# Engine order planned by free SBUF places and new DMA landing times, and the transposed input of the second block fetched from the SP queue

## The chip, the cores and the metric

The kernel runs on one core of a Trainium2 chip. The metric is device time in microseconds (us) of one execution. Three runs of the kernel before gave a median of 1719.25 us (1719.18 to 1719.7).

## What is computed

Two transformer blocks run one after the other on 512 tokens of width 2048, all in float32. The first block puts 16 meta tokens in front (528 rows), takes an RMS norm, multiplies by a 2048-row input weight, runs eight heads of grouped attention with rotary angles and eight heads of differential attention, gates both, multiplies by an output weight, norms and adds the residual. The second block norms that sum and multiplies by its own input weight; its columns feed eight heads of stick-breaking attention and a linear recurrence (convolution, two gates, a scan), and an output weight and a residual follow:

```
x = first_block(x, meta_tokens, ...)       # h + rmsnorm(y @ w_out)
return second_block(x, ...)                # proj = rmsnorm(x) @ w_in_2 ; ... ; h + y @ w_out_2
```

## The kernel before, in words

**Matmuls.** A float32 operand is split into two float32r parts, high and low, and a product is three passes over them (`PASSES`, L667). `split` (L417 to L419) makes the parts: ACT casts the high part (L418), DVE subtracts for the low one (L419). All matmuls are recorded on one line, L451.

**Weights.** Weights of the plain products (`in_wp`) come in units of two halves, 512 KB a half, through three raw places (`wraw`) and three split places (`wsp`). `load_next` (L570) issues the load of a half from the SP queue (L580) and splits it. Most other projections use a seven-product scheme over a pair of column blocks (`seven`, `produce`, `sum_up`), whose weights are loaded by SP (L616) and partly summed by a DMA that POOL issues (L625).

**Between the blocks.** `side_pair` (L1291) norms two token tiles, transposes them on TensorE, scales them into `xg` (L1316), stores `xg` to the DRAM tensor `x2d` with a DMA of POOL (L1319) and splits it into `big`. Then `v_half` (L1696) multiplies two token tiles at a time by the value weights of the second block, plain units; its result goes through ACT (L1703) to the DRAM tensor `vd` by a DMA of POOL (L1704). Meanwhile `side_x2` (L938) prepares the operands of the seven-product scheme: for each of six pairs (j, 6 + j) it fetches two transposed 128 x 512 blocks of `x2d` into tiles of the tag `e` (L945), 256 KB each in pieces of 512 B, subtracts quarters on DVE (L951 to L954) and splits the results with ACT and DVE into `x23b` and `x1sb`. The fetch of pair j + 1 is written ahead of the work on pair j. The tag `e` has six places, which many other steps use too. Later, L1782 fetches blocks of `x2d` of half that size from the SP queue.

**The order of the work.** TensorE's order comes from generators that `run` interleaves by a clock of their own. For the other engines (ACT, DVE, POOL and the SP queue) the class `Plan` records every instruction with its cost and its predecessors, gives each a due time counted back from the TensorE instruction that needs it (`order`, L253), runs a list scheduler over all engines and lays the result down as a fixed order on each engine. An engine works strictly in that order: an instruction that waits holds up all that stand behind it. `own` (L128) ties a tile to the tag whose places it uses; in the kernel before, the first use of a tile has all users of the tile `bufs` places back in its tag as hard predecessors:

```
if len(h) > bufs:
    before.append(h[-1 - bufs])
...
cost, busy = (1300.0 + nb / 260.0, 60.0) if e == "SP" else (3300.0 + nb / 220.0, 870.0)
```

The tile allocator itself gives a tile any place of its tag that is free.

Of the kernel before, what the change touches and what calls it, by code (L numbers as in the profile page):

```python
# [16 lines left out]
P = 128  # L17
# [93 lines left out]
class Plan:  # L111
# [2 lines left out]


    HOP = 40.0
    LEAD, SETTLED = 8000.0, 60000.0
    TABLES = ({"Tanh", "Exp", "Square", "Identity", "Copy"}, {"Exp", "Ln", "Abs", "Square", "Identity", "Copy"},
              {"Sqrt", "Square", "Identity", "Copy"})

    def __init__(self):
        self.ins, self.engine, self.cost, self.busy, self.func, self.preds = [], [], [], [], [], []
        self.nbytes, self.adds = [], []
        self.parts, self.users, self.after_of, self.history = {}, {}, {}, {}
        self.turn_of, self.opened, self.newest, self.begun = {}, {}, {}, []
        self.behind, self.names = None, {}

    def own(self, ap, tag, bufs, following=()):  # L128

        h = self.history.setdefault(tag, [])  # L130
        self.turn_of[ap.name] = tag
        h.append(ap.name)
        before = list(following)
        if len(h) > bufs:
            before.append(h[-1 - bufs])
        self.after_of[ap.name] = before
        self.users[ap.name] = []
        return ap

# [38 lines left out]
    def __call__(self, ins):  # L178
        op, e = type(ins).__name__[4:], str(ins.engine).split(".")[-1]
        aps = [[o.bass_ap for o in group if hasattr(o, "bass_ap")] for group in (ins.outs, ins.ins)]  # L180
        if not type(ins).__name__.startswith("Inst") or (not aps[0] and op != "LoadActFuncSet"):
            return
        i = len(self.ins)
        preds, begun = set(), set()
        if self.behind is not None and str(self.behind.engine) == str(ins.engine):
            preds.add(self.behind.name)
        preds = {self.names[p] for p in preds} if preds else set()
        pe = e == "PE"
        for writes, group in ((False, aps[1]), (True, aps[0])):
            for ap in group:  # L190
                name = ap.name
                if name.startswith("in_") or name.startswith("out_"):
                    continue
                for t in self.after_of.pop(name, ()):
                    preds.update(self.users.get(t, ()))
                if name in self.turn_of:
                    tag = self.turn_of.pop(name)
                    if tag in self.newest:
                        begun.add(self.newest[tag])
                    self.newest[tag] = self.opened[name] = i  # L200
                elif name in self.opened:
                    begun.add(self.opened[name])
                if name in self.users:
                    self.users[name].append(i)
                span = self._span(ap)
                w = writes or str(ap.space) == "PSUM"
                parts = self.parts.setdefault(name, {})
                lo, hi = span[0][0], span[-1][1]
                for key in [k for k in parts if k[0][0] < hi and lo < k[-1][1]]:
                    if not any(a < d and c < b for a, b in key for c, d in span):  # L210
                        continue
                    writer, readers = parts[key]
                    if writer is not None:
                        preds.add(writer)
                    if w:
                        preds.update(readers.values())
                        if key == span or (len(span) == 1 and lo <= key[0][0] and key[-1][1] <= hi):
                            del parts[key]
                if w:
                    parts[span] = [i, {}]  # L220
                else:
                    parts.setdefault(span, [None, {}])[1]["PE" if pe else i] = i
        preds.discard(i)
        if pe:
            preds = {j for j in preds if self.engine[j] != "PE"}
            begun = {j for j in begun if self.engine[j] != "PE"}
        self.begun.append(begun - preds - {i})
        n = max([ap.free_size() for g in aps for ap in g] or [1])
        self.nbytes.append(0)
        self.adds.append(str(getattr(ins, "cce_op", "")).endswith("add"))  # L230
        if op == "DMACopy":
            nb = 4
            for _, k in aps[0][0].ap:
                nb *= k
            self.nbytes[-1] = nb
            cost, busy = (1300.0 + nb / 260.0, 60.0) if e == "SP" else (3300.0 + nb / 220.0, 870.0)
        elif op == "LoadActFuncSet":
            cost = busy = 1283.0
        else:
            if op == "TensorScalarPtr" and getattr(ins, "is_tensor_tensor_scan", False):  # L240
                op = "TensorTensorScan"
            if pe:
                n = aps[0][0].free_size()
            cost, busy = self._costs(ins, e, op, n, str(aps[1][0].dtype) if aps[1] else "")
        self.ins.append(ins)
        self.names[ins.name] = i
        self.engine.append(e)
        self.cost.append(cost)
        self.busy.append(busy)
        self.func.append(str(getattr(ins, "func", "")).split(".")[-1] if op == "Activation" else op)  # L250
        self.preds.append(preds)

    def order(self):  # L253

        N = len(self.ins)
        succs = [[] for _ in range(N)]
# [7 lines left out]
        t, due = 0.0, [math.inf] * N  # L264
# [3 lines left out]
                t += self.busy[i]  # L268
        for i in range(N - 1, -1, -1):
            if self.engine[i] != "PE":  # L270
                due[i] = min([due[j] for j in succs[i]] + [t]) - self.cost[i] - self.HOP
                due[i] = min([due[i]] + [due[j] for j in heirs[i]])
        left = [len(p) + len(b) for p, b in zip(self.preds, self.begun)]
        at = [0.0] * N
        clock = {e: 0.0 for e in self.engine}
        ready = {e: [] for e in clock}
# [8 lines left out]
        def wanted(i):  # L285
            now = due[pe[min(pe_next, len(pe) - 1)]]
            return not self.nbytes[i] or now > self.SETTLED or due[i] - self.LEAD <= now

        eager = False
        while count < N:  # L290
            best = None
            for e, r in ready.items():
                if e == "PE":
                    if pe_next == len(pe) or left[pe[pe_next]]:
                        continue
                    i = pe[pe_next]
                    s = max(clock[e], at[i])
                else:
                    r = [i for i in r if eager or wanted(i)]
                    if not r:  # L300
                        continue
                    s = max(clock[e], min(at[i] for i in r))
                if best is None or s < best[0]:
                    best = (s, e)
            if best is None:
# [3 lines left out]
            if e == "PE":  # L309
                i = pe[pe_next]  # L310
                pe_next += 1
            else:
                def rank(i):
                    other = e == "Activation" and self.ins[i] and self.switch(i, table[0])
                    return due[i] + (4000.0 if other else 0.0)

                i = min((i for i in ready[e] if at[i] <= s and (eager or wanted(i))), key=rank)
                eager = False
                ready[e].remove(i)
            if e == "Activation":  # L320
# [6 lines left out]
            clock[e] = s + self.busy[i]  # L327
            end = s + self.cost[i]
            if self.nbytes[i]:
                lat = 1300.0 if e == "SP" else 2400.0  # L330
                pipe = max(clock[e] + lat / 2, pipe) + self.nbytes[i] * (1.9 if self.adds[i] else 1.0) / 300.0
                end = pipe + lat / 2
            self.fin[i] = end
            done[e].append(i)
            count += 1
            for j, when in [(j, end + self.HOP) for j in succs[i]] + [(j, s) for j in heirs[i]]:
                left[j] -= 1
                at[j] = max(at[j], when)
                if not left[j] and self.engine[j] != "PE":
                    ready[self.engine[j]].append(j)  # L340
# [10 lines left out]
def hybrid_two_block_kernel(ctx: ExitStack, tc: tile.TileContext, wp, wq, wc, xT, xtok, par, lvec, cst, rg, pg, lruw, out):  # L351
    nc = tc.nc
# [61 lines left out]
    def blocks(ap, n=P):  # L414
        return ap.rearrange("p (a b) -> p a b", b=n)
# [522 lines left out]
    def side_x2():  # L938
# [3 lines left out]
        def fetch(j):  # L942
            x = et(NTOK), et(NTOK)
            for t, kt in zip(x, (j, KS + j)):
                pool.dma_start(blocks(t), x2d[kt // 8].rearrange("t p c -> p t c")[:, :, kt % 8 * P : (kt % 8 + 1) * P])  # L945
            return x

        a, b = fetch(0)
# [1035 lines left out]
```

## Time and profile before

| | us |
|---|---|
| median of three runs | 1719.25 |
| the profiled execution | 1719.21 |
| span of its trace, first to last instruction | 1717.4 |
| TensorE (PE) busy | 1668.4 |
| DVE busy | 1207.1 |
| ACT busy | 945.4 |
| POOL busy | 188.2 |

The mean granted clock of TensorE is 0.992 of full speed. An engine's time in the span is busy time plus idle time; in the rows a figure in square brackets is the idle time just before an instruction and what ended it. "issue" stands for time in which the engine waited for nothing that the profile shows. A DMA's instruction on its queue is short; "to landing" runs from the issue to the last byte's semaphore.

### The profile page before, as it was taken

The page shows a single profiled execution, that of the slowest core. Times are in us where ns is not written, and L with a number is a line of the kernel's source. Part 1 is how long each engine was busy: PE and PEld are TensorE (multiplying, and loading weights), DVE is VectorE, ACT ScalarE, POOL GpSimd, SP SyncE. Part 2 cuts the span into 40 slices and gives each one's busy share as a digit, 9 for nine tenths or more (in the row PEclk, how much of TensorE's full clock was granted, in tenths as well). Part 3 has the DMA queues.
Part 4 walks back from the last instruction along what each step waited for, and adds up shares of the span by engine and source line. Part 5 has one row for each costly group of instructions (what it writes and reads, how often), then busy time and mean ns, then how long its engine had stood idle before and what let it go on. Part 6 is the DMA issues. An engine that isn't in the chain of part 4 may idle for free.

```text
span 1717.4 us, 28307 instructions
## 1 busy us (share of the span) xinstructions
PE 1668.4 (97%) x10840; PEld 1512.0 (88%) x10840; DVE 1207.1 (70%) x2073; ACT 945.4 (55%) x1581; POOL 188.2 (11%) x217
## 2 busy tenths in 40 slices
PE   8999999999999999999999879999999999999999
PEld 8789999999999999888887659999998888888887
DVE  4874787776889888873577647898875466886433
ACT  6554566664767766673455434666643366775311
POOL 0111121111122222100000111111100000000000
PEclk9999999999999999999999989999999999999999
DMA  8535856767665656544577666666667322434233
GB/s 301 174 124 141 209 136 165 175 158 168 145 145 140 153 129 144 149 132 134 200 249 257 233 188 163 154 188 151 190 173 239 114 85 86 141 93 126 83 92 129
DMA packets 104552, 273.01 MB, mean 159 GB/s; under 512 B 11728, under 2 KB 19024, under 8 KB 102736
## 3 DMA queue, kind: packets, MB, share of 16 engines
q1 hardware_dynamic: 86944, 221.90, 39.7%
q0 software_dynamic: 17472, 49.29, 16.2%
q8 instruction: 85, 1.39, 0.3%
q14 instruction: 51, 0.42, 0.1%
HBM read 241.79 MB, written 29.36 MB: 158 GB/s over the span
## 4 chain that ended last, share of the span: by engine, by line
PE 63%; DVE 5%; DMA 3%; issue 3%; ACT 2%; POOL 0%; SPq 0%; DVEq 0%; ACTq 0%; POOLq 0%
PE pj L451 56%; PE pmt L451 2%; PE pss L451 2%; DVE wsp L419 2%; DMA wraw<-in_wp 1%; PE ptt L454 1%; DMA wraw<-in_wq 1%; PE bank L451 1%; ACT wsp L418 1%; PE pmt L454 1%; DMA e<-x2d 0%; DMA vd<-e 0%; PE pss L454 0%; DVE ar L1276 0%; POOL e L945 0%
## 5 line engine op out<-in xcount | busy, mean ns | idle before, releaser
L451 PE MATMUL pj<-wsp,big 128*128 128x512 f32 x3072 | 745.6, 400 | 23.9 <-ACT wsp L418 18.3
L451 PEld LDWEIGHTS pj<-wsp,big 128*128 128x128 f32 x3072 | 575.7, 190 | 159.1 <-ACT wsp L418 20.6
L419 DVE TENSOR_TENSOR wsp<-wraw,wsp 128x768 fp32r<-128x768 f32 (+3 forms) x459 | 464.1, 1016 | 231.7 <-ACT wsp L418 224.5
L418 ACT CAST wsp<-wraw 128x768 fp32r<-128x768 f32 (+3 forms) x459 | 401.6, 878 | 385.8 <-PE pj L451 291.3
L451 PE MATMUL pj<-big,wsp 128*128 128x264 f32 (+2 forms) x4224 | 539.2, 283 | 10.6 <-ACT wsp L418 7.2
L451 PEld LDWEIGHTS pj<-big,wsp 128*128 128x128 f32 x4224 | 518.6, 189 | 13.6 <-ACT wsp L418 7.5
L625 POOL DMA_DIRECT2D wraw<-in_wq x104 | 90.8, 883 | 631.1 <-DVE wsp L419 496.4
L451 PE MATMUL pj<-x,wsp 128*128 128x264 f32 x720 | 100.8, 287 | 3.2 <-DVE wsp L419 1.9
L451 PEld LDWEIGHTS pj<-x,wsp 128*128 128x128 f32 x720 | 92.4, 188 | 4.8 <-DVE wsp L419 2.5
L451 PE MATMUL pj<-x1s,wsp 128*128 128x264 f32 (+1 forms) x576 | 78.0, 285 | 1.9 <-DVE e L1760 1.9
L418 ACT CAST pt<-ptt 128x512 fp32r<-128x512 f32 (+2 forms) x96 | 50.7, 528 | 51.5 <-PE ptt L454 51.2
L419 DVE TENSOR_TENSOR pt<-ptt,pt 128x512 fp32r<-128x512 f32 (+2 forms) x96 | 59.6, 621 | 25.9 <-ACT pt L418 25.1
L451 PE MATMUL pss<-kk,qq 128*128 128x264 f32 x448 | 72.1, 289 | 3.6 <-DVE vtail L999 1.9
L451 PEld LDWEIGHTS pj<-x1s,wsp 128*128 128x128 f32 x576 | 72.9, 188 | 2.2 <-DVE e L1760 2.1
L451 PE MATMUL pmt<-pt,vv 128*128 128x256 f32 (+1 forms) x528 | 69.3, 279 | 0.0
L451 PEld LDWEIGHTS pmt<-pt,vv 128*128 128x128 f32 x528 | 67.2, 188 | 1.5
L1231 ACT ACTIVATE e<-e,sm 128x528 f32<-128x528 f32 x64 | 47.2, 737 | 38.2 <-DVE sm L1228 37.9
L451 PEld LDWEIGHTS pss<-kk,qq 128*128 128x128 f32 x448 | 61.4, 188 | 6.1 <-PE ptt L454 2.3
L451 PE MATMUL pj<-y,wsp 128*128 128x256 f32 x432 | 55.6, 282 | 0.0
L451 PEld LDWEIGHTS pj<-y,wsp 128*128 128x128 f32 x432 | 53.4, 189 | 0.0
L454 PE MATMUL ptt<-ident,e 128*128 128x128 f32 x336 | 52.5, 273 | 0.0
L1228 DVE CUSTOM_DVE_ANT_0 e<-pss,ar 128x528 f32<-128x528 f32 x64 | 44.9, 702 | 6.0 <-PE pss L451 5.8
(285 smaller groups left out, 1549.8 us busy)
## 6 DMA issues: line engine op xcount, KB each, us to landing
wraw<-in_wp SPq DMA_DIRECT2D x167, 512.0 KB, 4.1
wraw<-in_wq SPq DMA_DIRECT2D x128, 384.0 KB, 3.9
wraw<-in_wq POOLq DMA_DIRECT2D x104, 384.0 KB, 5.2
wraw<-in_wc SPq DMA_DIRECT2D x64, 256.0 KB, 2.8
gated<-e SPq DMA_DIRECT2D x40, 256.0 KB, 3.2
e<-in_xT SPq DMA_DIRECT2D x28, 264.0 KB, 4.2
early<-in_xtok SPq DMA_DIRECT2D x4, 1024.0 KB, 8.1
e<-yd SPq DMA_DIRECT2D x16, 256.0 KB, 4.0
```

The costliest lines, as they stand in the source:

```text
L418: act.copy(hi, src)
L419: dve.tensor_tensor(lo, src, f(hi), ALU.subtract)
L451: _queue(nc.tensor.matmul(out, lhsT, rhs, start=start, stop=stop).ins, cost)
L454: _queue(nc.tensor.transpose(out, in_, identity).ins, 110.0)
L625: pool.dma_start(pair_raw[(p, r)], wq[p, q], accum_op=ALU.add)
L1228: dve.tensor_tensor_reduce(out=halves(x), in0=s[:, :, :HL], in1=halves(bias[:, b0 : b0 + L]), scale=1.0, scalar=3e38, op0=ALU.add, op1=ALU ...
L1231: act.activation(x, x, AF.Exp, scale=-1.0, bias=nm, accum_out=l[:, m : m + 1])
```

## The change

Four things are edited.

- Places: the first use of a tile no longer has the users of the tile `bufs` back as predecessors. The scheduler keeps, for each tag, the times at which its places come free (a place is taken at a tile's first use and freed 40 ns after its last user ends); an instruction that opens a tile starts no earlier than the first free place, and not at all while none is free. The due times still look at the tile `bufs` back (`soft`).
- DMA model: a DMA of SP lands after 1900 ns of latency (1300 before), one of POOL after 2000 ns (2400 before), 700 ns more where the target is DRAM, plus the bytes over a shared pipe at 300 bytes per ns as before.
- Margin: whoever needs a DMA's data is planned up to 700 ns after its modelled landing, where its due time leaves room (half of the slack).
- `side_x2` issues its twelve fetches (L945) from SP instead of POOL.

```diff
@@ class Plan
-    LEAD, SETTLED = 8000.0, 60000.0
+    LEAD, SETTLED, MARGIN = 8000.0, 60000.0, 700.0
...
@@ own
-        before = list(following)
+        self.after_of[ap.name] = list(following)
+        self.room[tag], self.tag_of[ap.name] = bufs, tag
         if len(h) > bufs:
-            before.append(h[-1 - bufs])
-        self.after_of[ap.name] = before
+            self.heir_of[ap.name] = h[-1 - bufs]
...
@@ __call__
+                    self.opens.setdefault(i, []).append(name)
+                    if name in self.heir_of:
+                        self.soft.setdefault(i, []).extend(self.users[self.heir_of[name]])
...
-            cost, busy = (1300.0 + nb / 260.0, 60.0) if e == "SP" else (3300.0 + nb / 220.0, 870.0)
+            lat = (1900.0 if e == "SP" else 2000.0) + (700.0 if str(aps[0][0].space) == "DRAM" else 0.0)
+            self.lat[i] = lat
+            cost, busy = (lat + nb / 260.0, 60.0) if e == "SP" else (lat + 870.0 + nb / 150.0, 870.0)
...
@@ order
-                due[i] = min([due[j] for j in succs[i]] + [t]) - self.cost[i] - self.HOP
+                due[i] = min([due[i], min([due[j] for j in succs[i]] + [t]) - self.cost[i] - self.HOP])
                 due[i] = min([due[i]] + [due[j] for j in heirs[i]])
+            for j in self.soft.get(i, ()):
+                if self.engine[j] != "PE":
+                    due[j] = min(due[j], due[i] - self.cost[j] - self.HOP)
+        free = {tag: [0.0] * n for tag, n in self.room.items()}
...
+        def slot(i):
+            t = 0.0
+            for name in self.opens.get(i, ()):
+                f = free[self.tag_of[name]]
+                t = max(t, min(f) if f else math.inf)
+            return t
...
-                    s = max(clock[e], min(at[i] for i in r))
+                    s = max(clock[e], min(max(at[i], slot(i)) for i in r))
+                    if s == math.inf:
+                        continue
...
-                i = min((i for i in ready[e] if at[i] <= s and (eager or wanted(i))), key=rank)
+                i = min((i for i in ready[e] if max(at[i], slot(i)) <= s and (eager or wanted(i))), key=rank)
...
-                lat = 1300.0 if e == "SP" else 2400.0
+                lat = self.lat[i]
...
+            for name in self.opens.get(i, ()):
+                f = free[self.tag_of[name]]
+                f.remove(min(f))
+            for name in tiles[i]:
+                live[name] -= 1
+                last[name] = max(last.get(name, 0.0), end + self.HOP)
+                if not live[name]:
+                    free[self.tag_of[name]].append(last[name])
...
+                if self.nbytes[i] and when > s:
+                    late = clock["PE"] - due[pe[min(pe_next, len(pe) - 1)]]
+                    when += min(max((due[j] + late - when) / 2, 0.0), self.MARGIN)
...
@@ side_x2, fetch
-                pool.dma_start(blocks(t), x2d[kt // 8].rearrange("t p c -> p t c")[:, :, kt % 8 * P : (kt % 8 + 1) * P])
+                nc.sync.dma_start(blocks(t), x2d[kt // 8].rearrange("t p c -> p t c")[:, :, kt % 8 * P : (kt % 8 + 1) * P])
```

## Rows read from the trace of the kernel before

**Rows 1.** The page, busy time, its share of the span and instructions.
```profile
span 1717.4 us, 28307 instructions
PE 1668.4 (97%) x10840; PEld 1512.0 (88%) x10840; DVE 1207.1 (70%) x2073; ACT 945.4 (55%) x1581; POOL 188.2 (11%) x217
```

**Rows 2.** Waits of PE, whole span: waiter, awaited: us in total, times, longest us.
```profile
PE pj L451 <- ACT wsp L418: 26.7, 9, 6.8
PE pj L451 <- DVE wsp L419: 7.0, 11, 1.6
```

**Rows 3.** Busy time by stretch: PE, PEld, DVE, ACT, POOL, PEclk, DMA share, GB/s.
```profile
0.00:50.00 50.00, 42.81 (x313) 41.18 (x314) 22.60 (x39) 32.47 (x47) 0.83 (x7) 1.00 0.83 307
...
1700.00:1717.00 17.00, 13.20 (x57) 10.35 (x56) 4.62 (x7) 1.05 (x1) 0.00 (x0) 0.97 0.24 93
```

**Rows 4.** The same view, stretches cut to the stages.
```profile
970.00:1020.00 50.00, 31.94 (x102) 22.60 (x101) 24.89 (x44) 16.10 (x24) 8.31 (x12) 0.80 0.48 147
1020.00:1044.00 24.00, 24.00 (x105) 19.42 (x105) 12.17 (x10) 11.02 (x13) 2.02 (x3) 1.00 0.70 208
...
720.00:730.00 10.00, 7.09 (x21) 5.09 (x20) 7.89 (x13) 7.75 (x13) 0.00 (x0) 0.66 0.58 190
895.00:915.00 20.00, 18.10 (x85) 14.27 (x84) 15.41 (x27) 9.38 (x13) 1.22 (x3) 1.00 0.90 353
```

**Rows 5.** Timeline of PE from 970 to 1020: start, us, instruction, idle before.
```profile
980.11 1.22 PE L451 MATMUL pj<-wsp,big 128*128 128x512 f32 x2 [6.78 <-ACT wsp L418]
...
996.23 1.22 PE L451 MATMUL pj<-wsp,big 128*128 128x512 f32 x2 [4.67 <-ACT wsp L418]
...
1015.82 1.22 PE L451 MATMUL pj<-wsp,big 128*128 128x512 f32 x2 [5.27 <-ACT wsp L418]
```

**Rows 6.** Waits of all engines from 955 to 1020.
```profile
ACT x1s L418 <- DVE e L951: 32.0, 6, 7.9
POOL e L945 <- issue: 29.2, 8, 5.9
DVE e L951 <- DMA e<-x2d: 26.5, 6, 6.4
...
POOL e L945 <- DMA vd<-e: 6.1, 1, 6.1
```

**Rows 7.** Timeline of POOL from 940 to 1050: first, one in the middle and last fetch.
```profile
959.25 0.78 POOL L945 DMA_DIRECT2D e<-x2d  x1 [0.37 <-PE pj L451]
...
976.92 0.76 POOL L945 DMA_DIRECT2D e<-x2d  x1 [2.96 <-issue]
...
1009.88 0.76 POOL L945 DMA_DIRECT2D e<-x2d  x1 [2.90 <-issue]
```

**Rows 8.** Line L945, its twelve fetches on POOL.
```profile
DMA to landing us min/median/max: 3.3/3.4/6.4
```

**Rows 9.** Fetches of half the size on SP: timeline at 1293 to 1300, line L1782.
```profile
1294.79 4.03 SPq L1782 DMA_DIRECT2D e<-x2d  x6
...
DMA to landing us min/median/max: 4.8/5.5/6.2
```

**Rows 10.** Tile wraw from 955 to 1020: durations in ns, min/median/max.
```profile
L419 DVE TENSOR_TENSOR wsp<-wraw,wsp x14: 1215/1218/1227, 954.7 to 1017.7; 128x1024 fp32r<-128x1024 f32 x14
...
L418 ACT CAST wsp<-wraw x13: 1037/1043/1053, 955.2 to 1016.2; 128x1024 fp32r<-128x1024 f32 x13
...
DMA to landing us min/median/max: 3.5/4.4/7.0
```

**Rows 11.** The page, DMA issues: count, KB each, median us to landing.
```profile
wraw<-in_wp SPq DMA_DIRECT2D x167, 512.0 KB, 4.1
...
wraw<-in_wq POOLq DMA_DIRECT2D x104, 384.0 KB, 5.2
```

**Rows 12.** Timeline of PE, the two longest gaps outside 970 to 1020 and the start.
```profile
722.54 0.73 PE L451 MATMUL pj<-wsp,big 128*128 128x512 f32 x1 [2.30 <-ACT big L418]
...
1234.81 2.42 PE L451 MATMUL pj<-x1s,wsp 128*128 128x256 f32 x18 [1.85 <-DVE e L1760]
```

More of the change, by code (lines that the diff above doesn't have):

```diff
@@ L122, in __init__ @@
         self.ins, self.engine, self.cost, self.busy, self.func, self.preds = [], [], [], [], [], []
-        self.nbytes, self.adds = [], []
+        self.nbytes, self.adds, self.lat = [], [], {}
         self.parts, self.users, self.after_of, self.history = {}, {}, {}, {}
@@ L126, in __init__ @@
         self.behind, self.names = None, {}
+        self.room, self.tag_of, self.heir_of, self.opens, self.soft = {}, {}, {}, {}, {}
     def own(self, ap, tag, bufs, following=()):
@@ L270, in order @@
             if self.engine[i] != "PE":
-                due[i] = min([due[j] for j in succs[i]] + [t]) - self.cost[i] - self.HOP
+                due[i] = min([due[i], min([due[j] for j in succs[i]] + [t]) - self.cost[i] - self.HOP])
                 due[i] = min([due[i]] + [due[j] for j in heirs[i]])
+            for j in self.soft.get(i, ()):
+                if self.engine[j] != "PE":
+                    due[j] = min(due[j], due[i] - self.cost[j] - self.HOP)
+        free = {tag: [0.0] * n for tag, n in self.room.items()}
+        live, last, tiles = {}, {}, [[] for _ in range(N)]
+        for name, us in self.users.items():
+            live[name] = len(set(us))
+            for i in set(us):
+                tiles[i].append(name)
+        def slot(i):
[4 more added lines that the diff above has]
+            return t
         left = [len(p) + len(b) for p, b in zip(self.preds, self.begun)]
@@ L296, in order @@
                     i = pe[pe_next]
-                    s = max(clock[e], at[i])
+                    s = max(clock[e], at[i], slot(i))
+                    if s == math.inf:
+                        continue
                 else:
@@ L301, in order @@
                         continue
-                    s = max(clock[e], min(at[i] for i in r))
+                    s = max(clock[e], min(max(at[i], slot(i)) for i in r))
+                    if s == math.inf:
+                        continue
                 if best is None or s < best[0]:
```

## The prediction

> **What bounds the kernel now.** I began with the page's busy times: TensorE works 1668.4 of 1717.4 us [rows 1], so the kernel is bound by TensorE and only the 49.0 us of its gaps, and what a lowered clock costs after them, can be won. The waits of PE come next: 26.7 us in nine gaps end with an ACT cast of a weight, 7.0 us in eleven with the DVE subtract behind it [rows 2]. So it is late weights, not late results, that stop TensorE.
>
> Busy time by stretch says where. The start holds 50 - 42.81 = 7.19 us of gaps and the tail 17 - 13.20 = 3.80 us, with 0.4 us after it [rows 3]; nothing in the change is aimed at either. One stage, 970 to 1020, holds 50 - 31.94 = 18.06 us [rows 4]. Everything else is 49.0 - 7.19 - 4.2 - 18.06 = 19.5 us, in gaps of at most 2.30 us [rows 12].
>
> That stage loses more than its gaps. From 1020 to 1044 TensorE does 105 of the same matmuls in 24 us, 4.375 a us, at a granted clock of 1.00; from 970 to 1020 it does 102, which at that rate need 23.3 us [rows 4]. The loss is 50 - 23.3 = **26.7 us**: 18.06 us of gaps and 8.6 us of matmuls run while the mean granted clock is 0.80, that is, partly at the lower of its two levels. Each us of gap here costs 26.7 / 18.06 = 1.48 us.
>
> Why there: three gaps of 6.78, 4.67 and 5.27 us end with a weight's cast [rows 5]. In that stretch ACT waits 32.0 us, in six waits, for DVE's L951 before its cast into x1s; DVE's L951 waits 26.5 us, in six, for the fetch of the transposed input [rows 6]. The weight's cast stands behind that cast in ACT's fixed order, its data long landed. And the fetches are late because POOL can't issue them faster: POOL sits 29.2 us in "issue" before them [rows 6], some 2.9 us before each one, with 0.76 us for the instruction: 3.66 us a fetch [rows 7]. The twelve take from 959.25 to 1009.88, 4.6 us apart on average, since POOL also waits once 6.1 us after the stores to vd [rows 6, 7].
>
> **The change part by part.**
>
> *The fetches move to SP.* What is removed: 12 x 3.66 = 44 us of POOL's issue. The two vd stores that stood among them, and those after, find POOL free. What is added on SP: six fetches of half the size were issued there in 4.03 us, 0.67 us each [rows 9]. The new ones have twice the pieces; between 0.67 us (issue does not grow) and 1.34 us (it grows with the pieces) I take 1.34 us, as on POOL it is the pieces that cost: 16 us in all, 2.7 us a pair, against 7.3 us. Landing was 3.4 us on POOL [rows 8] and 5.5 us for the half-size ones back to back on SP [rows 9]; one pair ahead of the work covers either.
>
> SP is not empty: 512 KB weight loads stand behind each fetch. A half serves 12 matmuls, 2.74 us at the full rate, and with three raw places a place has 8.2 us for its round: landing 4.4, cast 1.04, subtract 1.22 [rows 10], with some 0.3 us for issue 7.0 us. Slack is 1.2 us. A fetch alone (1.34 us) makes a load 0.1 us late, a pair in one go 1.5 us. Six pairs cost 1 us (spread) to 9 us (in one go) of gaps, at 1.48 that is 1 to 13 us; I take 6, nearer the lower end, because the planner places each fetch by its due time. The gain of the stage is 26.7 - 6 = **20.7 us**, with ends 13.7 and 25.7. The other cover is DMA capacity: the stage's bytes fill 0.48 of 50 us; the same bytes in 29 us fill 0.82, below the 0.90 at which a neighbouring stretch still lost only 1.9 us [rows 4].
>
> *Places and the DMA model.* TensorE's order does not come from the plan, so no matmul is added, moved or removed, and no other engine gets an instruction more or less except the fetches. What changes is the order on ACT, DVE, POOL and SP for the whole span. The old model lets a 512 KB load of SP land 1.3 + 1.75 = 3.05 us after issue, the new one 3.65; measured are 4.1, and 4.4 in the stage. An accumulate of 384 KB on POOL, weighted 1.9, is 4.9 before and 4.5 after, without the 0.87 us of issue; measured 5.2 [rows 10, 11]. So SP's landing comes nearer to the trace, POOL's no nearer. Places counted from first to last use let a step open a tile as soon as any place is free, as the allocator does; the plan may now fetch earlier, and may also fill places that a more urgent step would have had. The trace of before shows none of this, so I bound it: the best would close all 19.5 us of gaps and the 2.4 us that the clock costs after the gap at 722 (0.34 of 7.09 us, [rows 4]); the worst opens as many again. I take a gain of **2 us**, near zero, because these gaps are short and of several kinds, and a new order makes new ones.
>
> *Margin.* It moves a consumer by at most 0.7 us and only where slack remains; I cost it at nothing. Its cover is that slack; without it a weight split comes up to 0.7 us later, inside the 1.2 us above.
>
> **Sum.** Against the profiled execution, 1719.21 us (1717.4 us of span and 1.8 around it; the median of the runs, 1719.25, is the same): 1719.2 - 20.7 - 2 = 1696.5, say **1697 us**.
>
> Against this stands a rule. The rows show that issuing is longer than moving: 3.66 us a fetch against a landing of 3.4 us [rows 7, 8]. The Trainium skill (DMA: Bandwidth & Descriptors, "Issuing engines are not separate DMA queues") says that the issuing engines share the same 16 DMA engines and that choosing another saves only the issue time, usually small beside the transfer. By that rule the stage would keep its pace, as in the second rival; here the trace contradicts "usually small".
>
> **The rivals.**
>
> 1. *SP is held by the fetches (slower).* SP works in order. A fetch that waits for an e place or for x2d's last store holds all weight loads behind it; on POOL only stores stood there. If each pair holds SP as long as POOL once waited, 6.1 us [rows 6], a load is 6.1 - 1.2 = 4.9 us late, 29.4 us of gaps over six pairs instead of 18.06: (29.4 - 18.06) x 1.48 = 17 us, so 1736 us. It decides from a hold of 18.06 / 6 + 1.2 = 4.2 us a pair. For it: three raw places and 1.2 us of slack. Against it: the plan now counts e places, and the fetch of pair j + 1 is due a pair ahead. Chance 0.10.
>
> 2. *The transfers, not the issue, set the pace.* If places allow only one pair in flight, a pair takes 2.7 us of issue and the longest landing, 6.2 us [rows 9]: 8.9 us against 2 x 4.6 = 9.2 today [rows 7]. That saves 0.3 x 6 = 1.8 us, with the clock 2.7: 1716.5 us; with partial overlap 1705 to 1716. For it: SP's fetches landed slower though smaller. Against it: POOL's second pair was issued at once behind the first, and its gaps name issue, not places, for 29.2 us [rows 6]. By the skill's rule this would be the outcome. Chance 0.20, most of it with partial overlap.
>
> 3. *The new order closes other gaps too.* If half of the 19.5 us and the 2.4 us go, and the stage keeps 1 us: 1719.2 - 25.7 - 12.2 = 1681 us; the case reaches from 1676 to 1690. For it: weights that are late because of their landing are what PE waits for elsewhere too [rows 2]. Against it: many causes, and the new POOL landing is no nearer. Chance 0.15.
>
> 4. *The change does not do what it says:* the plan may lay the fetches down at the places where POOL's came, held by steps ahead of them, and gains and losses elsewhere cancel: 1719 us. Chance 0.03.
>
> **How the numbers follow.** My forecast, 1690 to 1705 us, has 0.52; the others 0.10, 0.20, 0.15 and 0.03. The predicted time is the forecast's own, 1697. The range 1682 to 1713 takes in the stage's ends (13.7 and 25.7 us), a third or so of the bounds elsewhere, two thirds of rival 2 and of rival 3; left out are rival 1, rival 4 and the far parts of the other two, about 0.2. A measurement of this kernel can tell 0.2%, 3.4 us, from no change. Faster by more than that is below 1715.8: 0.52 + 0.15 + 0.20 = 0.87; within it 0.03; slower 0.10.
>
> **What would show it.** In the changed profile the fetches stand on SP, POOL has no "issue" of 2.9 us before fetches, DVE's six waits of 26.5 us for e<-x2d fall below 6 us, the gaps of PE in the stage add up to some 4 us and the granted clock there is near 1.00; the 102 matmuls take about 29 us instead of 50. Step one is wrong if SP's weight loads wait behind L945 and PE's waits for weight casts stay near 18 us. The twelve issues should take 8 to 16 us of SP; longer issues, or landings above 6.2 us, would be rival 2. Step two is wrong if the gaps outside the stage, now 19.5 us, end below 12 or above 25 us. The whole is wrong if a new gap of over 5 us stands in a stage that has none today.

## The result and the profile after

The changed kernel takes **1694.29 us** (median of 5 runs, 1691.02 to 1696.23), against 1719.25 us (1716.74 to 1720.97, 5 runs beside it): a ratio of **0.9851, 95% interval 0.9835 to 0.9868**. The forecast was 1697 us. The profiled execution took 1696.23 us, with a span of 1694.5 us.

The first two lines of the page are its span and busy times, as [rows 1].

```profile
span 1694.5 us, 28288 instructions
...
PE 1663.9 (98%) x10840; PEld 1511.1 (89%) x10840; DVE 1206.4 (71%) x2073; ACT 944.1 (56%) x1581; POOL 183.3 (11%) x205
```

TensorE has the same 10840 matmuls. Its gaps add up to 1694.5 - 1663.9 = 30.6 us, where they were 49.0, and its busy time is 4.5 us shorter; less of it runs at the lower clock, as the granted clocks of the stretches below show. POOL has lost twelve instructions, the fetches. (Every line of the kernel behind the planner stands 38 lines lower now: the matmul L451 is L489, the split L418/L419 is L456/L457, the fetch L945 is L983, the weight load L580 is L618.)

The waits of PE over the whole span (us in total, times, longest us), as [rows 2]:

```profile
PE pj L489 <- ACT wsp L456: 11.9, 7, 5.9
...
PE pss L492 <- issue: 3.1, 1, 3.1
```

The wait for ACT's casts has fallen from 26.7 to 11.9 us, and half of what is left (5.9) is the one at the start of the kernel. A new line stands below: one gap of 3.1 us at L492, put down to "issue".

Busy time by stretch, columns as in [rows 3]. The stretches are the start, an early one, 603 to 780 and the whole stage. The stage is cut by work: from its first plain matmul to the next stage's first, 269 matmuls in every kernel.

```profile
0.00:50.00 50.00, 41.84 (x303) 40.91 (x304) 22.40 (x37) 30.21 (x43) 0.83 (x7) 1.00 0.84 294
...
80.00:90.00 10.00, 9.20 (x30) 7.18 (x31) 8.14 (x14) 3.23 (x7) 2.39 (x2) 0.66 0.19 54
...
603.00:780.00 177.00, 175.74 (x1269) 165.19 (x1269) 148.66 (x284) 123.33 (x242) 26.70 (x21) 1.00 0.57 149
...
952.80:1017.70 64.90, 62.62 (x270) 49.39 (x269) 43.90 (x61) 33.50 (x42) 3.75 (x7) 1.00 0.80 247
```

The same two later stretches in the kernel before; its stage ran from 956.4 to 1044.4:

```profile
603.00:780.00 177.00, 169.46 (x1199) 157.87 (x1198) 145.77 (x275) 119.22 (x232) 26.14 (x21) 0.98 0.54 139
956.40:1044.40 88.00, 69.94 (x269) 53.48 (x268) 44.75 (x61) 32.10 (x41) 12.92 (x19) 0.88 0.60 183
```

The stage takes 64.9 us instead of 88.0, with 2.3 us of gaps instead of 18.1 and a granted clock of 1.00 instead of 0.88. At the rate of [rows 4], 4.375 matmuls a us, 269 need 61.5 us, so 3.4 us of loss are left.

Following the same matmul through both kernels gives the account of the whole span. The lead of the changed kernel is -6.0 us at the first of the 32 matmuls `pmt<-ptail,vtail` (199.0 us before, 205.0 after), -6.0 still at the 24th of them (603.1 and 609.1), **+3.6** at the last (781.9 and 778.3), +26.7 at the stage's end (1044.4 and 1017.7), +23.2 at the first bank matmul (1380.9 and 1357.6), and +22.9 at the end. So: 6 us lost early, 9.6 won from 609 to 778, 23.1 won in the stage, 3.8 lost behind it, most of it by 1357. Without the stage, that is a loss of 0.2 us.

The timeline of PE (start us, us, instruction, idle before it) shows the gap behind most of the early loss, and the longest of the stage.

```profile
80.81 1.30 PE L492 MATMUL pss<-ident,early 128*128 128x128 f32 x5 [3.15 <-issue]
...
968.03 22.23 PE L489 MATMUL pj<-wsp,big 128*128 128x512 f32 x92 [0.88 <-DVE wsp L457]
```

The gap of 3.15 us costs more than itself: in the stretch 80 to 90 the granted clock is 0.66, and 30 matmuls keep TensorE busy for 9.20 us.

The queue of SP from 945 to 985, as a timeline, shows the fetches among the weight loads; the last line is of the line L983.

```profile
953.02 2.81 SPq L983 DMA_DIRECT2D e<-x2d  x4
957.84 3.22 SPq L618 DMA_DIRECT2D wraw<-in_wp  x3
962.79 3.44 SPq L983 DMA_DIRECT2D e<-x2d  x4
968.01 5.08 SPq L618 DMA_DIRECT2D wraw<-in_wp  x3
975.41 2.94 SPq L983 DMA_DIRECT2D e<-x2d  x3
...
DMA to landing us min/median/max: 3.7/4.5/7.7
```

The first four fetches go out in 2.81 us, 0.70 us each, where two on POOL stood 3.66 us apart [rows 7]. No fetch landed in under 3.7 us, so these four were under way together. All twelve are issued from 953.0 to 978.9, in 26 us instead of 51, and well ahead of the work.

### The profile page after: what moved, and what is told of

Its sections match the earlier page's. It is cut to its first block, busy times and chain, and to the rows that moved or that the text cites. A ratio compares the mean times of both kernels' runs of the same rounds, so it can differ in the third digit from the quotient of the medians.

```text
span 1694.5 us, 28288 instructions
## 1 busy us (share of the span) xinstructions
PE 1663.9 (98%) x10840; PEld 1511.1 (89%) x10840; DVE 1206.4 (71%) x2073; ACT 944.1 (56%) x1581; POOL 183.3 (11%) x205
## 4 chain that ended last, share of the span: by engine, by line
PE 65%; DVE 5%; issue 3%; DMA 3%; ACT 2%; POOL 0%; ACTq 0%; DVEq 0%; POOLq 0%
PE pj L489 57%; PE pmt L489 2%; PE pss L489 2%; DVE wsp L457 2%; PE ptt L492 1%; DMA wraw<-in_wq 1%; PE bank L489 1%; DMA wraw<-in_wp 1%; ACT wsp L456 1%; PE pmt L492 1%; PE pss L492 0%; DMA e<-yd 0%; DVE e L1266 0%; DVE e L1435 0%; DMA gated<-e 0%
## 5 line engine op out<-in xcount | busy, mean ns | idle before, releaser
L489 PE MATMUL pj<-wsp,big 128*128 128x512 f32 x3072 | 738.0, 397 | 5.9 <-DVE wsp L457 3.0
L489 PEld LDWEIGHTS pj<-wsp,big 128*128 128x128 f32 x3072 | 571.3, 189 | 137.7 <-DVE wsp L457 5.8
L457 DVE TENSOR_TENSOR wsp<-wraw,wsp 128x768 fp32r<-128x768 f32 (+3 forms) x459 | 464.3, 1017 | 236.0 <-ACT wsp L456 228.4
L456 ACT CAST wsp<-wraw 128x768 fp32r<-128x768 f32 (+3 forms) x459 | 400.3, 877 | 389.2 <-PE pj L489 284.1
L489 PE MATMUL pj<-big,wsp 128*128 128x264 f32 (+2 forms) x4224 | 542.3, 284 | 12.3 <-ACT wsp L456 9.5
L489 PEld LDWEIGHTS pj<-big,wsp 128*128 128x128 f32 x4224 | 521.5, 190 | 15.5 <-ACT wsp L456 10.2
L489 PE MATMUL pj<-x,wsp 128*128 128x264 f32 x720 | 100.9, 287 | 1.6 <-DVE wsp L457 1.0
L489 PEld LDWEIGHTS pj<-x,wsp 128*128 128x128 f32 x720 | 92.4, 188 | 3.1 <-DVE wsp L457 1.9
L456 ACT CAST pt<-ptt 128x512 fp32r<-128x512 f32 (+2 forms) x96 | 50.7, 528 | 56.6 <-PE ptt L492 56.2
L489 PE MATMUL pj<-x1s,wsp 128*128 128x264 f32 (+1 forms) x576 | 78.7, 286 | 2.2 <-DVE e L1798 2.2
L457 DVE TENSOR_TENSOR pt<-ptt,pt 128x512 fp32r<-128x512 f32 (+2 forms) x96 | 59.6, 620 | 25.0 <-ACT pt L456 24.6
L489 PEld LDWEIGHTS pj<-x1s,wsp 128*128 128x128 f32 x576 | 73.5, 190 | 2.5 <-DVE e L1798 2.4
L489 PE MATMUL pss<-kk,qq 128*128 128x264 f32 x448 | 72.0, 288 | 0.9 <-ACT e L1192 0.5
L489 PE MATMUL pmt<-pt,vv 128*128 128x256 f32 (+1 forms) x528 | 69.3, 279 | 0.0
L489 PEld LDWEIGHTS pmt<-pt,vv 128*128 128x128 f32 x528 | 67.2, 188 | 1.6
L489 PEld LDWEIGHTS pss<-kk,qq 128*128 128x128 f32 x448 | 61.5, 189 | 3.1 <-issue 0.9
L489 PE MATMUL pj<-y,wsp 128*128 128x256 f32 x432 | 55.6, 282 | 0.0
L489 PEld LDWEIGHTS pj<-y,wsp 128*128 128x128 f32 x432 | 53.4, 189 | 0.0
L492 PE MATMUL ptt<-ident,e 128*128 128x128 f32 x336 | 52.5, 273 | 0.0
```

Source lines behind the costliest of these rows:

```text
L456: act.copy(hi, src)
L457: dve.tensor_tensor(lo, src, f(hi), ALU.subtract)
L489: _queue(nc.tensor.matmul(out, lhsT, rhs, start=start, stop=stop).ins, cost)
L492: _queue(nc.tensor.transpose(out, in_, identity).ins, 110.0)
```

## The experiments

Ratios are against the kernel before, run beside them; in brackets stands the 95% interval. A time marked "one run" is a single one and has no ratio.

**The move of the fetches alone.** One line of the kernel before; the planner and its prices stay.

```diff
-                pool.dma_start(blocks(t), x2d[kt // 8]...
+                nc.sync.dma_start(blocks(t), x2d[kt // 8]...
```

> The kernel before with one edit: the twelve fetches of side_x2 go out from SP, the plan stays as it was. Theory A (the move of the fetches is the gain, the plan is worth little): the stage from the first plain matmul after the last side_pair transposes to the first seven-product matmul takes about 65 us instead of 88, so 1697 us, within 1693 to 1702; DVE's waits for e<-x2d fall from 26.5 to below 6 us. Theory B (a plan that models landings and places is needed, since with the old one SP's weight loads stand behind waiting fetches): the stage still takes 75 us or more and the time is 1706 us or above.

Measured: 1694.70 us (1692.82 to 1696.29), **0.9858 (0.9840 to 0.9876)**. Its stage by stretch:

```profile
956.80:1019.40 62.60, 61.75 (x269) 49.55 (x268) 44.57 (x61) 32.61 (x41) 3.68 (x7) 1.00 0.80 256
```

The interval holds the ratio of the whole change, 0.9851. As far as these runs can tell, that one line brings all of the gain; the stage alone wins 88.0 - 62.6 = 25.4 us. DVE waits 2.4 us for e<-x2d from 950 to 1000, where it waited 26.5.

**The planner's part alone:** the changed kernel with the fetches back on POOL (the same line, the other way round).

> The changed kernel with the fetches put back on POOL: the new plan alone. Theory A: POOL still needs 3.6 us a fetch, the stage stays at 85 to 90 us with some 18 us of gaps, and the time is 1714 to 1722 us. Theory B: the new plan puts the weights' casts ahead of the late fetches, the stage's gaps fall to 10 us or less, and the time is 1708 us or below.

Measured: 1715.99 us, **0.9980 (0.9969 to 0.9992)**. The stage by stretch, and from the timelines its longest gap on PE and a fetch on POOL:

```profile
951.00:1035.30 84.30, 68.47 (x270) 53.13 (x269) 44.41 (x61) 33.18 (x42) 12.95 (x19) 0.90 0.60 191
```

```profile
972.50 13.11 PE L489 MATMUL pj<-wsp,big 128*128 128x512 f32 x42 [8.70 <-ACT wsp L456]
```

```profile
970.85 0.76 POOL L983 DMA_DIRECT2D e<-x2d  x1 [2.81 <-issue]
```

Counting places and modelling landings anew leaves a pause of 2.8 us or more before the fetches, and with it the stage's gaps: 84.3 - 68.47 = 15.8 us. Alone this part is worth some 3.5 us; on top of the move nothing shows.

**What POOL's pause hangs on: the pieces.** Two kernels of before fetch the same 256 KB in 128 pieces of 2 KB instead of 512 pieces, one on POOL and one on SP. They leave out the transposition of the input.

```diff
-                pool.dma_start(blocks(t), x2d[kt // 8]...
+                pool.dma_start(t, x2d[kt // 8, kt % 4][:, :NTOK])
```

> The kernel before, where each of the twelve fetches on POOL takes a contiguous block of the same 256 KB in 128 pieces of 2 KB instead of 512 pieces of 512 B; it leaves out the transposition of the second block's input and so computes something else from there. If POOL's issue time is made by the number of pieces: the gap before each fetch falls from 2.9 us to about 0.7 us, the twelve fetches take 20 us or less, and the stage loses most of its 18 us of gaps. If it is a fixed cost of each DMA of POOL: the gap stays at 2.9 us and the stage at 88 us.

Measured: 1695.22 us (one run); the stage takes 63.2 us. POOL's timeline, and the line L945 itself (durations in ns, min/median/max):

```profile
953.18 0.54 POOL L945 DMA_DIRECT2D e<-x2d  x1 [0.16 <-PE pj L451]
953.96 1.16 POOL L945 DMA_DIRECT2D e<-x2d  x2 [0.24 <-DMA wraw<-in_wp]
```

```profile
L945 POOL DMA_DIRECT2D e<-x2d x12: 536/538/550, 953.2 to 980.1; - x12
```

Two fetches follow each other within 1.16 us; the pause is gone. The twelve still take 27 us, not the 20 that were expected, as they wait for other engines' work. With longer pieces the engine need not be changed at all.

What the pause is, the kernel before shows. Two of its last fetches on POOL, and the landing of each of them alone:

```profile
999.57 0.77 POOL L945 DMA_DIRECT2D e<-x2d  x1 [2.94 <-DVE wsp L419]
1006.23 0.75 POOL L945 DMA_DIRECT2D e<-x2d  x1 [5.88 <-issue]
```

```profile
DMA to landing us min/median/max: 6.4/6.4/6.4
...
DMA to landing us min/median/max: 3.4/3.4/3.4
```

The fetch of 999.57 landed 6.4 us later, and the next one started 0.3 us after that; this one landed after 3.4 us, and again the next one, of 1009.88 [rows 7], started 0.3 us behind. So it goes for ten of the eleven fetches that follow another in this kernel, 0.30 to 0.37 us behind the landing. The eleventh stands behind two stores to vd and waited for them. The planner's part alone shows the same, ten of eleven, 0.30 to 0.37 us. So "issue" is here the wait for the landing of the fetch before: POOL has one fetch of 512 pieces under way at a time. With 128 pieces the three above, of 953.18 to 954.58, were under way together, and landed after 6.9 to 8.1 us. Why POOL holds back a fetch of 512 pieces is not shown.

The long pieces on SP (`nc.sync.dma_start` in that line):

> The kernel with the fetches on SP and the old plan, in 128 pieces of 2 KB each instead of 512 of 512 B; it leaves out the transposition of the second block's input. If pieces still cost something on SP: each issue gets shorter (0.7 us to about 0.35 us when back to back), weight loads land earlier than 5.6 us, and the stage goes from 62.6 to 61.5 us. If SP doesn't pay for pieces: stage and time as with 512 B pieces, 62 to 63 us and 1692 to 1697 us.

Measured: 1694.21 us (one run), a time as expected if SP doesn't pay for pieces, but a stage of 64.7 us, longer than either side expected. The line L945 on SP:

```profile
L945 SPq DMA_DIRECT2D e<-x2d x12: 319/383/818, 947.7 to 976.8; - x12
...
DMA to landing us min/median/max: 2.6/5.2/7.6
```

And the same line with 512 pieces, in the run of the move alone, which has the same plan:

```profile
L945 SPq DMA_DIRECT2D e<-x2d x12: 359/425/913, 958.4 to 983.3; - x12
...
DMA to landing us min/median/max: 2.7/5.4/7.1
```

With four times the pieces the median instruction takes 425 ns instead of 383, and the median landing is 5.4 us instead of 5.2. So on SP the pieces cost next to nothing in these runs, in issue or in landing. On POOL they decide whether one fetch or several are under way.

**Is it the transfers?** In the kernel before with the fetches on SP, one fixed pair of tiles is used for all six pairs, so that no pair can be fetched before the last one has been read.

```diff
+        keep = et(NTOK), et(NTOK)
...
-            x = et(NTOK), et(NTOK)
+            x = keep
...
-            later = fetch(j + 1) if j + 1 < KS else None
...
-            if later:
-                a, b = later
+            if j + 1 < KS:
+                a, b = fetch(j + 1)
```

> The kernel with the fetches on SP and the old plan, but with one pair of tiles for all six pairs, so that a fetch waits until the work on the pair before is done: no pair ahead. The second rival (one pair in flight sets the pace): a pair takes issue, landing and work one after the other, about 9 us, the stage is back above 80 us and the time is 1710 us or above. The forecast's view: six such pairs need 54 us, less than the 61.5 us that the stage's 269 matmuls need, so a pair ahead is a comfort and not a need: the stage stays below 70 us, 1693 to 1703 us.

Measured: 1696.72 us (1695.35 to 1702.27), **0.9857 (0.9840 to 0.9875)**. The stage by stretch, and its timeline:

```profile
958.20:1019.40 61.20, 61.20 (x269) 49.72 (x268) 43.77 (x60) 32.29 (x41) 2.71 (x5) 1.00 0.81 259
```

```profile
958.53 0.93 SPq L947 DMA_DIRECT2D e<-x2d  x2
...
968.11 1.26 SPq L947 DMA_DIRECT2D e<-x2d  x2
...
969.32 50.28 PE L451 MATMUL pj<-wsp,big 128*128 128x512 f32 x216
```

One pair in flight, some 10 us a pair, and TensorE does not stop once: 216 matmuls stand in one row of 50.28 us. So a pair ahead is not needed. And the pairs come no faster here than on POOL before, 9.2 us a pair. So it is not their pace alone that stops TensorE. What is left is the order of the other engines' work: in this run the plan knows that a pair waits for the one before, as they share their tiles, and can order the casts for it. That this is the reason is argued, not shown.

**Would it do to tell the plan what POOL's issue costs?** The kernel before, the fetches on POOL, priced as the prediction reads the trace: 2.79 us later and 3.66 us of POOL each.

```diff
+            if e != "SP" and aps[1][0].name.startswith("x2d"):
+                cost, busy = cost + 2790.0, 3660.0
```

> The kernel before, fetches still on POOL, with one edit: its old plan counts 3.66 us of POOL for each of the twelve fetches instead of 0.87 us. Theory A (POOL is too slow for twelve fetches of 512 pieces; only the move helps): the stage stays above 80 us and the time above 1712 us. Theory C (the plan's wrong price is the cause: ACT and DVE are ordered for fetches that come too early, and a plan that knows the true pace puts the weights first; 12 x 3.66 = 44 us fits into the 61.5 us that the matmuls need): the stage falls to 62 to 68 us and the time to 1692 to 1701 us.

Measured: 1712.58 us (1709.99 to 1718.42), **0.9960 (0.9948 to 0.9973)**, between the theories. The stage by stretch, then POOL's fetches and a gap of PE:

```profile
959.20:1037.20 78.00, 68.11 (x270) 52.54 (x268) 43.95 (x60) 32.03 (x42) 12.09 (x18) 0.93 0.65 203
```

```profile
962.01 0.78 POOL L947 DMA_DIRECT2D e<-x2d  x1 [0.37 <-PE pj L453]
...
1006.64 0.77 POOL L947 DMA_DIRECT2D e<-x2d  x1 [3.02 <-DVE wsp L421]
1013.78 0.75 POOL L947 DMA_DIRECT2D e<-x2d  x1 [6.37 <-issue]
1017.48 0.76 POOL L947 DMA_DIRECT2D e<-x2d  x1 [2.95 <-DVE x1s L421]
```

```profile
1002.76 0.74 PE L453 MATMUL pj<-wsp,big 128*128 128x512 f32 x2 [2.90 <-ACT wsp L420]
```

The longest gap falls from 6.78 to 2.90 us, which fits a plan that no longer puts weights' casts so far behind the late ones. But the stage still takes 78.0 us, and the twelve fetches stand 5.0 us apart on average (962.0 to 1017.5), slower than the 3.66 us planned. The pauses are those of the kernel before: the fetch of 1006.64 landed after 6.8 us, and the next one started 0.3 us later, behind a pause of 6.37 us. So the price was still too low, as it left the landings out. It wins about 7 us (the profiled execution, of 1716.7 us, only 2.5). Whether a plan that waits for each landing would win the rest with the fetches on POOL was not run.

**The planner's new parts, one by one.** The changed kernel without the margin:

```diff
-    LEAD, SETTLED, MARGIN = 8000.0, 60000.0, 700.0
+    LEAD, SETTLED, MARGIN = 8000.0, 60000.0, 0.0
```

> The changed kernel with MARGIN 0. Theory A (the margin is worth nothing that can be measured): 1691 to 1698 us, and the gap of 3.15 us near 80 us with the lowered clock behind it is still there, since it comes from the new landing times. Theory B (the margin makes that early gap, because it pushes DVE's work on the first block's keys back): the gap is gone, and the time is 1686 to 1691 us. Theory C (the margin is what closed gaps between 600 and 760 us): they come back, 1697 to 1702 us.

Measured: 1699.05 us (1694.88 to 1699.74), **0.9868 (0.9850 to 0.9887)**. PE's timeline:

```profile
84.81 0.79 PE L492 MATMUL pss<-ident,early 128*128 128x128 f32 x5 [1.52 <-issue]
...
621.09 0.73 PE L489 MATMUL pss<-kk,qq 128*128 128x264 f32 x4 [1.04 <-DVE vtail L1037]
```

```profile
85.00:90.00 5.00, 5.00 (x18) 3.85 (x17) 4.44 (x10) 2.19 (x4) 0.00 (x0) 0.66 0.31 73
```

The early gap of 3.15 us is gone, though the granted clock still falls, to 0.66 from 85 to 90 us, and gaps of about 1 us between 600 and 760 are back. So the margin causes the one and closes the others, and the sum can't be told from nothing.

Without the margin and with the old landing times:

```diff
+            self.lat[i] = 1300.0 if e == "SP" else 2400.0
-            cost, busy = (lat + nb / 260.0, 60.0) if e == "SP" else (lat + 870.0 + nb / 150.0, 870.0)
+            cost, busy = (1300.0 + nb / 260.0, 60.0) if e == "SP" else (3300.0 + nb / 220.0, 870.0)
```

> The changed kernel with the old DMA model (1300 and 2400 ns of latency, the old costs) and no margin: places and SP fetches alone are new. Theory A: within 4 us of the changed kernel, 1690 to 1698 us. Theory B (landing times planned nearer to the measured ones carry the gain): late weights return, PE's waits for weight casts and subtracts go from 18.6 to over 25 us and the time is 1701 us or above.

Measured: 1692.49 us (1685.55 to 1694.52), **0.9840 (0.9821 to 0.9859)**: the new landing times are not needed for the gain. With the old landing times and the margin:

> The changed kernel with the old DMA costs and latencies but with the margin of 700 ns. If the margin helps and the new landing times hurt: no early gap, fewer gaps between 600 and 760 us, 1685 to 1691 us. If neither matters: 1690 to 1696 us, as without the margin (1692.5).

Measured: 1703.18 us (1700.78 to 1705.47), **0.9897 (0.9879 to 0.9915)**, as neither side expected. PE's timeline:

```profile
77.92 1.30 PE L493 MATMUL pss<-ident,early 128*128 128x128 f32 x5 [2.90 <-issue]
...
1160.21 3.73 PE L490 MATMUL pj<-y,wsp 128*128 128x256 f32 x18 [2.94 <-DVE e L1806]
```

The early gap is back, and there are new ones. The parts don't add: the margin costs about 10 us here (0.9897 against 0.9840 of 1719 us) and nothing that can be told on the new landing times.

**The margin later.** The changed kernel, with the margin only from the 150th us of the plan on:

```diff
-                if self.nbytes[i] and when > s:
+                if self.nbytes[i] and when > s and clock["PE"] > 150000.0:
```

> The changed kernel with the margin only after 150 us of TensorE's planned time. If the early gap of 3.15 us and the lowered clock behind it come from the margin, and nothing else changes: no gap above 1 us between 70 and 95 us, and 1688 to 1691 us. If orders elsewhere change with it: 1690 to 1699 us.

Measured: 1690.26 us (1689.04 to 1692.25), **0.9830 (0.9814 to 0.9845)**, the shortest median of all. PE's timeline and two stretches:

```profile
83.36 0.79 PE L492 MATMUL pss<-ident,early 128*128 128x128 f32 x5 [1.53 <-issue]
```

```profile
80.00:90.00 10.00, 8.47 (x38) 6.50 (x38) 9.61 (x18) 4.91 (x8) 1.20 (x1) 1.00 0.33 103
...
603.00:780.00 177.00, 176.15 (x1251) 164.96 (x1250) 146.94 (x279) 122.35 (x236) 27.66 (x21) 1.00 0.56 147
```

One gap is 0.5 us longer than expected, and the clock stays at 1.00 from 80 to 90 and 603 to 780 keeps its gaps closed. It beats the kernel before clearly. Against the changed kernel its interval still overlaps (0.9835 to 0.9845), and the two were not run side by side.

## Why the prediction was right, point by point

**Where and why.** The stage held, and so did the chain from the late fetch over DVE and ACT to the weight's cast. With the fetches issued early (the move alone), or in long pieces on the same engine, the gaps before the weights' casts go. With 512 pieces on POOL they stayed or only shrank, in both plans that were tried. In the changed kernel from 950 to 995, what stood behind the late fetch has shrunk, and no wait of DVE for e<-x2d is listed [rows 6]:

```profile
ACT x1s L456 <- DVE e L989: 4.4, 5, 1.7
...
PE pj L489 <- DVE wsp L457: 1.3, 2, 0.9
...
PE pj L489 <- ACT wsp L456: 0.9, 1, 0.9
```

What did not hold is the reading of POOL's time. "POOL can't issue them faster" and "3.66 us a fetch" put the 2.9 us before each fetch down to issuing it. The trace has them as the wait for the fetch before to land: 3.66 us are a landing of some 3.4 and 0.3 us. The instruction itself takes 0.76 us. The move helps because several fetches are under way together on SP, which the prediction doesn't say. Its gain came out all the same, since by either reading the twelve are done sooner from SP; that much of the agreement is luck.

**The move, 20.7 us.** Measured 23.1 in the changed kernel and 25.4 alone, within the ends 13.7 and 25.7. The mis-sized term is the price of a fetch on SP: "I take 1.34 us, as on POOL it is the pieces that cost". It costs 0.70 us in the first four, near the lower bound of 0.67 us from the half-size fetch [rows 9]; what holds on POOL for pieces does not hold on SP. The loss that remains is 3.4 us, or 1.1 in the move alone (62.6 - 61.5), not 6. But the price doesn't explain this by itself. The same working took 4.4 us for a weight's landing, and in the changed stage, from 953 to 1018, the line L618 shows more:

```profile
DMA to landing us min/median/max: 3.6/5.6/6.7
```

With 5.6 us the round of a raw place takes 8.2 us and its slack of 1.2 us is gone. By the prediction's own sum, twelve fetches of 0.70 us would then open 8.4 us of gaps, an estimate; 2.3 were measured. So that round is too strict a limit; what covers the loads instead is not shown. The clock came with the gaps, as the 1.48 us for each us of gap said: 18.1 - 2.3 = 15.8 us of gaps fewer are 23.1 us less, 1.46.

**Places and the DMA model, 2 us.** Measured: -0.2 outside the stage, made of 9.6 us won from 609 to 778 and 9.8 us lost at the start (6.0) and behind the stage (3.8). The sizes cancel as the step said ("a new order makes new ones"). The forecast's 22.7 us and the 22.9 measured agree so well by luck: the stage gave 2.4 us more than forecast, the rest 2.2 us less. The gaps outside the start, stage and tail are about 15.6 us, between the bounds of 12 and 25, and none exceeds 5 us.

**The margin, nothing.** In the sum it can't be told from nothing; its cover was wrong. It said that the margin moves a consumer only where slack remains. The gap of about 3 us near 80 us comes with the margin, under both landing times (3.15 and 2.90 us), and without it no gap there exceeds 1.53 us. That fits a plan that counts slack where the run has none; the slack itself was not measured.

**The rivals.** *SP held by the fetches* had to hold SP for 4.2 us a pair. The waits of SP from 950 to 1000 show a longest one of 2.3 us for a fetch, and 7.7 us in all, 1.3 us a pair:

```profile
SPq L983 <- DMA vd<-e: 3.9, 2, 2.3
SPq L983 <- DVE ar L992: 1.7, 1, 1.7
SPq L983 <- DVE e L990: 1.2, 1, 1.2
SPq L983 <- PE pmt L489: 0.9, 1, 0.9
```

*The transfers set the pace* was nearer the truth for POOL than the forecast, since each fetch there waited for a landing, but its outcome did not come: on SP a landing is no shorter (a median of 5.4 us in the move alone, 3.4 on POOL), but several are under way, and even one pair at a time was enough. The Trainium skill (DMA: Bandwidth & Descriptors, "Issuing engines are not separate DMA queues") says that starting DMAs from several engines saves only the time to initiate them, which is usually small beside the DMA. The trace agrees with "small", 0.76 us on POOL beside a landing of 3.4, where the prediction said that it contradicts it; it does not agree with "only", as the move also saved the waits for landings, and these were what the stage paid for.

*The new order closes other gaps* was half right: 603 to 780 has 1.3 us of gaps instead of 7.5, paid for elsewhere. *The change doesn't do what it says* falls with the fetches on SP.

## What to carry to other kernels

Where a DMA of many short pieces that GpSimd issues has "issue" ahead of it, compare its start with the landing of the one before. If the one follows the other each time, the DMAs go one by one, and a plan has to price them by their landings. Give many short pieces to SP, or make the pieces longer. Where an in-order engine's late cast holds back a cast that is not late, ask first what makes the late one late, and whether the plan knew, before improving the planner. And run the one-line part of a change alone: here it brought, as far as the runs can tell, all of what a rewrite of the planner came with.

## What the runs showed of the hardware that was not expected

- On POOL a 256 KB fetch in 512 pieces starts 0.30 to 0.37 us after the landing of the one before (3.3 to 6.4 us after its start), so one is under way at a time; the profile puts the wait down to "issue". In 128 pieces up to four were under way, at 0.54 us of instruction each. On SP up to four were under way with 512 pieces.
- Short pieces hardly lengthened issue or landing on SP: 425 ns and 5.4 us (medians) with 512, 383 ns and 5.2 us with 128.
- One gap of 3.15 us in a stretch that had none as long was followed by a granted clock of 0.66 over 10 us. Behind a gap of 1.53 us it stayed at 1.00 in one kernel (the margin later), and behind one of 1.52 us at the same matmuls it fell to 0.66 over 5 us in another (no margin). So the length of that gap does not decide it alone; what does is not shown.
- Planned at 3.66 us each, POOL's fetches came 5.0 us apart, with pauses of up to 6.37 us, as their landings took up to 6.8 us.
